# The last build of G in an encoder layer: its first load in four pieces, every second U block cut in two, 110 blocks ahead instead of 108

## Chip, cores, metric
The kernel runs on one core of one Trainium2 chip. The metric is the device time of one execution in microseconds, the median of the runs. The engines are named as in the profile: PE (TensorE, matmul), PEld (its weight loads), DVE (VectorE), ACT (ScalarE), POOL (GpSimd), SP (SyncE). A q behind the name means the engine's sequencer, which issues DMAs and waits.

## The reference
One layer of a post-norm encoder with 512 tokens of width 1024: layer norm, two kinds of attention, a second norm, and then the part that this case is about, a product-key expert layer (PEER) with 16384 experts:

```python
def one_chunk(xb):
    q = (xb @ w_q).reshape(PEER_CHUNK, PEER_HEADS, PEER_KEY_DIM)
    s1 = jnp.einsum('thd,kd->thk', q[..., :half], sub_keys[0])
    s2 = jnp.einsum('thd,kd->thk', q[..., half:], sub_keys[1])
    ...
    idx = (e1 * PEER_N_KEYS + e2).reshape(PEER_CHUNK, PEER_HEADS * PEER_TOPK)
    g = jax.nn.softmax(cv.astype(jnp.float32), axis=-1).reshape(PEER_CHUNK, -1).astype(xb.dtype)
    u = u_table[idx]
    hpre = jnp.einsum('td,ted->te', xb, u)
    act = g * jax.nn.gelu(hpre, approximate=False)
    return jnp.einsum('te,ted->td', act, v_table[idx])
```

Each token picks 128 experts. Its output is the sum of their rows of V, each weighted with a routing weight g times the gelu of the product of the token with the expert's row of U. A gate and a last norm follow.

## The kernel before, in words
**Three kinds of tokens.** The first 128 tokens are done by gathers: GpSimd fetches the picked rows of U, and later of V, one per token and pick, by indirect DMA, and VectorE multiplies them (`rows` at line 1170, `fetch_u` and `gather_v` at lines 1517 to 1536). The other 384 tokens are done densely: for all experts the activation is made and multiplied with V, and G, a matrix of routing weights with zeros where an expert wasn't picked, masks it. Of these 384, the 128 of chunk 1 (called own, NGC = 1) get their products with U by gathers too (`own_rows`), so the dense product with U runs over N_U = 256 tokens, and that with V over 384.

**Blocks.** The experts lie in 128 blocks of 128. A block of U is 512 KB. LEAD = 108 blocks of U are multiplied ahead of the loop, in FP32 (`lead_block`, line 1281: 8 matmuls of 128x256 against `whole`, the sum of the two parts of the turned tokens). Results of blocks below SPILL = 96 go to DRAM (`ge_dram`) and come back in the loop; the last ones stay in SBUF, KEPT_K of them in a pool of the gate's tiles (`leave_u`, line 1264) and the rest in the eight buffers `ge`. The remaining blocks of U are multiplied in the loop (`expert_in`, line 845): the block is loaded, split into a high part (a ScalarE copy to FP32R) and a low part (a VectorE subtraction), and 24 matmuls sum three products of parts (`mm3`, line 128).

**Building G.** For chunks 2, 3 and last chunk 1 `build_g` (line 1085) makes 128 tokens of G, in 16 steps of eight tokens: one-hots on VectorE and ScalarE, their products on PE, and ScalarE copies the sums to a stage `g_st`. A stage of 32 tokens is sent to `g_dram` in four stores (`send`, line 1068), issued from ScalarE. Four such slices belong to each chunk, 12 to all (NTG). Of the last chunk slices 0 and 1 are sent; 2 and 3 stay. The first eight blocks' worth of G for the loop is `first_g` (line 1446): its slices 0 to 3 are copied by ScalarE out of the last build's stages, its slices 4 to 11 are loaded back from `g_dram` by SyncE, in one load of 1 MB that is issued ahead of the last build. Just before it all stores that are still open are sent in a row (line 1444).

**Order of the work.** Ahead of the loop every engine's order is written out by hand. A planner keeps a balance: each build or side step returns its time on VectorE, `run_pe` (line 1076) multiplies it with PACE = 1.1 and deals out that much of PE's own work (`pe_work`: U blocks, the gate), whose pieces have planned prices (PRODUCT_U, 0.436 for one of the eight products of a block). During the last build 26 side rows (`beside`, line 1200: gathers of the first chunk, and two early blocks of V, cut into the free half of `hTh` and `hTl`) run between the build's steps. U blocks come through four buffers (three `raw`, one `raw_u`); SyncE loads the next when PE has finished with a buffer. What is left of PE's work after the build runs at line 1495, before the loop's own matmuls.

**The loop** (line 1564) takes 128 steps, blocks 96 to 127 first and then 0 to 95. Step n loads the block of V, splits it, multiplies G with the gelu results (line 1598), splits that, and adds 18 matmuls of 128x512 to six accumulators (`expert_out`, line 1546). Steps 8 to 27 also make a block of U (`block_of_u`, line 1478). Between the steps 231 remaining gather steps are dealt out by a key (lines 1626 and 1627): a step with a block of U counts 1, one without 0.57. G comes in tiles for eight steps; a tile is loaded in four pieces (`load_g`, line 1463), in steps 3 to 6 of a group of eight early in the loop and in steps 6 and 7 later:

```python
if n % GB == (GB // 2 - 1 + q if n < KEPT + 128 - LEAD + 4 else GB - 2 + q // 2):
    gt_next = load_g(n // GB * GB + GB, 3 - q if n < GB else q, gt_next, q == 0)
```

The functions that the change touches, as the profile's line numbers have them:

Of the kernel before, what the change touches and what calls it, by code (L numbers as in the profile page):

```python
# [15 lines left out]
OP = mybir.AluOpType  # L16
# [15 lines left out]
N_S = 128  # L32
# [1 line left out]
GT = 32  # L34
G_PARTS = 4
GB = 8
LEAD = 108
SPILL = 96
KEPT = 8
KEPT_K = 4  # L40
FIRST = 40
PACE = 1.1
AHEAD = 14.0
# [5 lines left out]
OWN_G_LATE = 4.0  # L49
SEAM = 7.0  # L50
WAIT = 8.4
OWN_LATE = 10.0
LATE = 0.57
OT = 8
W_SCALE = 32768.0
G_SPLIT = 1.0
# [23 lines left out]
def tile_encoder_layer(ctx: ExitStack, tc: tile.TileContext, A: dict, out: bass.AP):  # L80
# [105 lines left out]
    def flat_of(t, i, n=1):  # L186

        return t.rearrange("p a b c -> p (a b c)")[:, i * T:(i + n) * T]
# [6 lines left out]
    def ps_tile(name, bufs=2):  # L195
        return ps6.tile([128, 512], F32, name=name, bufs=bufs)
# [871 lines left out]
    def send():  # L1068

        if parts:  # L1070
            g, t, x = parts.pop(0)
            n = 128 // G_PARTS
            nc.scalar.dma_start(g_dram[g][:, x * n * GT:(x + 1) * n * GT],
                                t[:, x * n:(x + 1) * n].rearrange("p i t -> p (i t)"))

    def run_pe(amount):
        nonlocal due
        due += amount * PACE
        while due > 0:
            done = next(pe_work, 1e9)  # L1080
            due -= done
        if due < -1e6:
            due = 0.0

    def build_g(c, e1, e2, gw):
# [55 lines left out]
        for q in range(128 // OT):  # L1141
            oh = bt.tile(wide, F16, name="oh_i")
            by_v = [128, 2 * np_ - OI_ACT, 128, 2]
            nc.vector.tensor_tensor(oh[:, OI_ACT:], pairs.unsqueeze(1).to_broadcast(by_v),
                                    keys[:, q].rearrange("p s (a b) -> p (s a) b", b=2)[:, OI_ACT:].unsqueeze(2)
                                    .to_broadcast(by_v), op=OP.is_equal)
            for i in range(2 * OI_ACT):
                nc.scalar.activation(oh[:, i // 2, :, i % 2], iota, AF.Abs, bias=ne[:, OT * q + i:OT * q + i + 1])
            nc.scalar.activation(oh[:, 0:OI_ACT], oh[:, 0:OI_ACT], AF.Relu, bias=1.0, scale=-1.0)
            if ahead:  # L1150
                sums = products(*ahead)
                due -= G_SPLIT
            yield SPLIT_OH
            oj = bt.tile([128, 2, np_, 128, 2], F16, name="oh_j")
            for part in range(2):
                nc.vector.tensor_tensor(oj[:, part], oh[:, np_:],
                                        wt[:, q, part].rearrange("p (a b) -> p a b", b=2).unsqueeze(2)
                                        .to_broadcast([128, np_, 128, 2]), op=OP.mult)
                if part == 0:
                    yield SPLIT_OJ  # L1160
            if ahead:
                leave(ahead[0], sums)
            ahead = (q, oh, oj)
            yield SPLIT_OJ
# [31 lines left out]
    v_cut = {}  # L1196

    v_homes = [[flat_of(t, 2 * x, 2) for t in (hTh, hTl)] for x in range(2)]

    def beside():  # L1200

        nonlocal due
        raw = []

        def cut(n):
            split(*v_homes[n], raw[n])
            v_cut[n] = v_homes[n]

        for k, x in enumerate(rows(i_sel[:, 0, :], h[0], hdot[:, 0, :], range(BESIDE))):
            if k == BESIDE - 12:  # L1210
                due -= SEAM
            if k in (BESIDE - 12, BESIDE - 5):
                n = len(raw)
                raw.append(rw.tile([128, D], F32, name="h_s" if n else "gb"))
                nc.sync.dma_start(raw[n], v_rows[(SPILL + n) * 128:(SPILL + n + 1) * 128, :])
            yield x
            if k == BESIDE - 4:
                cut(0)
                yield 1.2
        cut(1)  # L1220
        yield 1.2


    PRODUCT_U, PRODUCT_G = 0.49 * N_U / 288, 0.69
    raws = []
    tasks = []
# [51 lines left out]

    last = []

    def lead_block():


        fill()
        if not raws:
            return
        nonlocal u_done
        i, raw = raws.pop(0)
        ps = psH.tile([128, 512], F32, name="hp") if gating else ps_tile("mm", 4)
        for k in range(8):  # L1290
            nc.tensor.matmul(ps[:, :N_U], raw[:, k], whole[:, k, :], start=(k == 0), stop=(k == 7))  # L1291
            if k == 3 and last:
                leave_u(*last.pop())
            if k % 2 and tasks:
                tasks.pop(0)()
            yield PRODUCT_U
        last.append((i, ps))
        u_done = i + 1
        if i in home_of:
            name, t = home_of[i]  # L1300
            idle[name].append(t)
# [95 lines left out]
    pe_work = gate_and_leads()  # L1397
    own, own_due = None, 0.0

    def run(steps, share=0.0, n=2):  # L1400

        nonlocal own_due
        for amount in steps:
            send()
            if amount is None:
                for _ in range(n if own else 0):
                    run_pe(next(own, 0.0))
                continue
            run_pe(amount)
            own_due += amount * share  # L1410
            while own and own_due > 0:
                x = next(own, None)
                if x is None or not x:
                    own_due = -1e9
                    break
                run_pe(x)
                own_due -= x

    with tc.manual_schedule(engines={nc.vector.engine, nc.scalar.engine, nc.tensor.engine, nc.sync.engine,
                                     nc.gpsimd.engine}):  # L1420
        fill()
        held = []
        run(route(NGC, held))
        own = own_rows(*held)
        run_pe(next(own))
        own_due = -OWN_LATE
        for c in range(NGC + 1, 4):
            res = []
            if c > NGC + 1:
                run(route(0, []), OWN)  # L1430
            run(route(c, res), OWN)
            if c > NGC + 1:
                run_pe(WAIT)
            run(build_g(c, *res), OWN)
        own_due = 1e9
        run([0.0], 1.0)
        side = beside()
        run_pe(next(side))
        for _ in own:
            pass  # L1440
        own = None
        run_pe(LAG)

        while parts:
            send()
        first_g = pX.tile([128, NTG, GB, GT], F32, name="gt1")
        nc.sync.dma_start(first_g[:, 128 // GT:].rearrange("p g i t -> p g (i t)"),
                          g_dram[128 // GT:, :, SPILL * GT:(SPILL + GB) * GT].rearrange("g p x -> p g x"))
        build = build_g(NGC, *held)
        next(build)  # L1450
        run_pe(next(side))
        own = side
        own_due = -OWN_G_LATE
        run(build, OWN_G)
        for x in own:
            run_pe(x)
        while parts:
            send()
        pb.close()
# [278 lines left out]
```

## Time and profile before

| | |
|---|---|
| median of 3 runs | 1489.74 us (1486.84 to 1492.28) |
| profiled execution, its own time | 1489.54 us |
| its span, first to last instruction | 1487.8 us |
| mean granted clock of TensorE | 0.996 |
| PE, DVE, ACT, POOL busy | 97%, 85%, 43%, 38% of the span |
| DMA | 453.82 MB, mean 305 GB/s |
| last build of G | about 810 to 878 us |
| first matmul of the loop's accumulators | 893.3 us |

The profile is one execution. A window row gives, for each engine, its busy time in the stretch with the number of instructions behind it, then the granted clock, the busy share of the 16 DMA engines and what they moved. An FP32 matmul leaves two entries in the trace, so a block of U ahead of the loop leaves 16. Entries of PE overlap, as a matmul's end is modelled: the distance of two starts tells the pace, not the duration of one. Times are microseconds from the start of the span.

### The profile page before, as it was taken

The page shows a single profiled execution, that of the slowest core. Times are in us where ns is not written, and L with a number is a line of the kernel's source. Part 1 is how long each engine was busy: PE and PEld are TensorE (multiplying, and loading weights), DVE is VectorE, ACT ScalarE, POOL GpSimd, SP SyncE. Part 2 cuts the span into 40 slices and gives each one's busy share as a digit, 9 for nine tenths or more (in the row PEclk, how much of TensorE's full clock was granted, in tenths as well). Part 3 has the DMA queues.
Part 4 walks back from the last instruction along what each step waited for, and adds up shares of the span by engine and source line. Part 5 has one row for each costly group of instructions (what it writes and reads, how often), then busy time and mean ns, then how long its engine had stood idle before and what let it go on. Part 6 is the DMA issues. An engine that isn't in the chain of part 4 may idle for free.

```text
span 1487.8 us, 22518 instructions
## 1 busy us (share of the span) xinstructions
PE 1450.2 (97%) x7693; PEld 1212.4 (81%) x7693; DVE 1268.5 (85%) x2736; ACT 638.4 (43%) x1203; POOL 570.7 (38%) x520
## 2 busy tenths in 40 slices
PE   9999999999999999999998999999999999999997
PEld 5788777788888878888887888988888888888775
DVE  7376786579998979998776987999899999999997
ACT  3355776243221554212555763444343333333433
POOL 1013110010014544344442435665555666666630
PEclk9999999999999999999999999999999999999999
DMA  7333340175239999999999999999999999999992
GB/s 255 99 111 92 97 128 30 29 245 170 100 125 351 334 416 415 405 324 336 392 416 410 376 396 369 415 417 417 401 393 411 412 412 411 412 412 412 411 362 85
DMA packets 196851, 453.82 MB, mean 305 GB/s; under 512 B 18945, under 2 KB 96897, under 8 KB 196738
## 3 DMA queue, kind: packets, MB, share of 16 engines
q1 hardware_dynamic: 119168, 211.72, 38.6%
q0 software_dynamic: 57984, 207.12, 35.5%
q10 hardware_dynamic: 19586, 33.57, 5.9%
q8 instruction: 60, 0.98, 0.2%
q14 instruction: 53, 0.43, 0.1%
HBM read 411.70 MB, written 37.75 MB: 302 GB/s over the span
## 4 chain that ended last, share of the span: by engine, by line
PE 56%; DMA 22%; DVE 9%; issue 6%; ACT 4%; POOL 3%; SPq 0%; ACTq 0%; DVEq 0%; POOLq 0%
PE acc L1551 16%; DMA raw<-in_v_rows_dram 11%; PE mm L1291 6%; PE hp L1291 5%; DMA ge_dram<-ge 4%; PE mm L129 4%; PE mm L131 4%; PE mm L130 4%; PE pj L129 3%; PE pj L130 3%; PE pj L131 3%; DMA v_raw<-in_v_rows_dram 3%; PE hp L129 1%; PE hp L131 1%; PE hp L130 1%
## 5 line engine op out<-in xcount | busy, mean ns | idle before, releaser
L110 DVE TENSOR_TENSOR wlo<-raw,whi 128x1024 fp32r<-128x1024 f32 (+4 forms) x113 | 131.5, 1164 | 45.7 <-ACT whi L110 45.4
L110 ACT CAST a_hi<-gt 128x384 fp32r<-128x384 f32 (+2 forms) x128 | 64.9, 509 | 242.4 <-DVE gt L1598 179.5
L110 ACT CAST whi<-raw 128x1024 fp32r<-128x1024 f32 (+4 forms) x113 | 113.0, 1001 | 106.9 <-PE mm L130 47.3
L1291 PE MATMUL mm<-whole,raw 128*128 128x256 f32 x672 | 153.1, 381 | 1.5 <-DMA raw<-in_uT_dram 1.5
L1174 POOL DMA_INDIRECT whi<-in_u_rows_dram,s_ix x51 | 64.2, 1259 | 218.5 <-DVE cand L994 129.7
L1551 PE MATMUL acc<-hTh,a_hi 128*128 128x512 f32 x456 | 141.8, 391 | 0.1
L1551 PE MATMUL acc<-hTl,a_hi 128*128 128x512 f32 x456 | 141.2, 390 | 0.0
L1551 PE MATMUL acc<-hTh,a_lo 128*128 128x512 f32 x456 | 140.9, 389 | 0.0
L1291 PEld LDWEIGHTS mm<-whole,raw 128*128 128x128 f32 x672 | 125.6, 190 | 17.9 <-DMA raw<-in_uT_dram 1.9
L1534 POOL DMA_INDIRECT gat<-in_v_rows_dram,i_sel x64 | 100.8, 1574 | 55.0 <-DVE base L1536 39.5
L110 ACT CAST hTh<-v_raw 128x1024 fp32r<-128x1024 f32 x74 | 77.8, 1051 | 55.9 <-PE acc L1551 23.1
L1551 PEld LDWEIGHTS acc<-hTl,a_hi 128*128 128x128 f32 x456 | 85.4, 188 | 18.3 <-DVE hTl L110 0.4
L1551 PEld LDWEIGHTS acc<-hTh,a_lo 128*128 128x128 f32 x456 | 85.4, 188 | 18.2 <-DVE a_lo L110 0.3
L1551 PEld LDWEIGHTS acc<-hTh,a_hi 128*128 128x128 f32 x456 | 84.1, 188 | 17.2 <-ACT a_hi L110 1.1
L110 DVE TENSOR_TENSOR hTl<-v_raw,hTh 128x1024 fp32r<-128x1024 f32 x74 | 90.2, 1219 | 6.4 <-ACT hTh L110 6.4
L1551 PE MATMUL acc<-wlo,a_hi 128*128 128x512 f32 x300 | 92.8, 390 | 0.2
L1551 PE MATMUL acc<-whi,a_hi 128*128 128x512 f32 x300 | 92.8, 391 | 0.1
L1551 PE MATMUL acc<-whi,a_lo 128*128 128x512 f32 x300 | 92.6, 390 | 0.0
L1174 POOL DMA_INDIRECT wlo<-in_u_rows_dram,s_ix x51 | 61.9, 1213 | 68.3 <-DVE s_dot L1176 56.0
L1519 POOL DMA_INDIRECT gat<-in_u_rows_dram,i_sel x52 | 69.1, 1329 | 45.2 <-DVE hdot L1525 34.1
L1536 DVE SCALAR_TENSOR_TENSOR base<-gat,hdot,base 128x1024 f32<-128x1024 f32 x64 | 82.0, 1281 | 1.0
L1273 ACT ACTIVATE ge<-mm 128x256 f32<-128x256 f32 x78 | 29.6, 380 | 110.4 <-PE mm L1291 100.5
(415 smaller groups left out, 3815.7 us busy)
## 6 DMA issues: line engine op xcount, KB each, us to landing
raw<-in_uT_dram SPq DMA_DIRECT2D x80, 512.0 KB, 7.8
v_raw<-in_v_rows_dram SPq DMA_DIRECT2D x78, 512.0 KB, 13.2
raw<-in_v_rows_dram SPq DMA_DIRECT2D x48, 512.0 KB, 13.8
g_dram<-g_st ACTq DMA_DIRECT2D x40, 512.0 KB, 12.1
ge_dram<-ge ACTq DMA_DIRECT2D x96, 128.0 KB, 7.0
ge<-ge_dram SPq DMA_DIRECT2D x96, 128.0 KB, 13.0
gt<-g_dram SPq DMA_DIRECT2D x30, 384.0 KB, 13.9
raw_u<-in_uT_dram SPq DMA_DIRECT2D x19, 512.0 KB, 7.8
```

What stands on the lines that cost most here:

```text
L110: cut = nc.scalar.copy(hi, src), nc.vector.tensor_tensor(lo, src, r32(hi), op=OP.subtract)
L129: nc.tensor.matmul(ps, a[0], b[0], start=start, stop=False)
L130: nc.tensor.matmul(ps, a[0], b[1], start=False, stop=False)
L131: nc.tensor.matmul(ps, a[1], b[0], start=False, stop=stop)
L1174: nc.gpsimd.indirect_dma_start(out=u[:], out_offset=None, in_=u_rows, in_offset=bass.IndirectOffsetOnAxis(ap=ix[:, k:k + 1], axis=0))
L1273: nc.scalar.activation(ge, ps[:, :N_U], AF.Gelu)
L1291: nc.tensor.matmul(ps[:, :N_U], raw[:, k], whole[:, k, :], start=(k == 0), stop=(k == 7))
L1519: nc.gpsimd.indirect_dma_start(out=u[:], out_offset=None, in_=u_rows, in_offset=bass.IndirectOffsetOnAxis(ap=i_sel[:, c, k:k + 1], axis=0))
L1534: nc.gpsimd.indirect_dma_start(out=u[:], out_offset=None, in_=v_rows, in_offset=bass.IndirectOffsetOnAxis(ap=i_sel[:, c, k:k + 1], axis=0))
L1536: nc.vector.scalar_tensor_tensor(base[c], u, hdot[:, c, k:k + 1], base[c], op0=OP.mult, op1=OP.add)
L1551: nc.tensor.matmul(acc[c][hf], a[:, cs], b[:, hf * 512:(hf + 1) * 512], start=(n == 0 and i == 0), stop=(n == 127 and i == 2))
```

## The change
Four edits.

First, the stores that are still open and the load of `first_g` are taken from before the last build. The load becomes four loads of two slices each (`load_first`), issued by SyncE at the build's steps 6, 7, 8 and 9; each first sends any store of the earlier chunks that is still open. The stores otherwise leave one per planner step.

Second, between the LAG work and the side row BESIDE - 7, every U block with an even number is split ahead of its matmuls into a high and a low part (ScalarE copy, VectorE subtraction), in the free halves of `hTh` and `hTl`, and multiplied with 24 FP32R matmuls instead of 8 FP32 ones. Its planned price per k is 0.36 instead of 0.436.

Third, LEAD is 110 instead of 108 and KEPT_K 6 instead of 4, so 18 blocks of U are left for the loop.

Fourth, each step of the last build deals out 0.1 less (MORE_G, times PACE).

```diff
-LEAD = 108
+LEAD = 110
-KEPT_K = 4
+KEPT_K = 6
+FIRST_G_AT = 6
+FIRST_PARTS = 4
+MORE_G = -0.1
+CUT_EVERY = 2
...
+    def load_first(x):
+        while parts and parts[0][0] >= N_S // GT:
+            send()
+        n = (NTG - N_S // GT) // FIRST_PARTS
+        g = slice(N_S // GT + x * n, N_S // GT + (x + 1) * n)
+        nc.sync.dma_start(first_g[:, g].rearrange("p g i t -> p g (i t)"),
+                          g_dram[g, :, SPILL * GT:(SPILL + GB) * GT].rearrange("g p x -> p g x"))
...
             nc.scalar.activation(oh[:, 0:OI_ACT], oh[:, 0:OI_ACT], AF.Relu, bias=1.0, scale=-1.0)
+            if c == NGC and 0 <= q - FIRST_G_AT < FIRST_PARTS:
+                load_first(q - FIRST_G_AT)
...
+            if k == BESIDE - 7:
+                cutting = False
...
+    def cut_next():
+        nonlocal n_cut
+        if cutting and len(raws) > 1 and raws[1][0] % CUT_EVERY == 0 and raws[1][0] not in in_parts:
+            i, raw = raws[1]
+            hi, lo = [t.rearrange("p (k n) -> p k n", n=128) for t in v_homes[n_cut % 2]]
+            n_cut += 1
+            in_parts[i] = hi, lo
+            tasks.extend([lambda: nc.scalar.copy(hi, raw), nothing, nothing, nothing,
+                          on_vector(1.2, lambda: nc.vector.tensor_tensor(lo, raw, r32(hi), op=OP.subtract))])
...
+        parts_u = in_parts.pop(i, None)
         for k in range(8):
-            nc.tensor.matmul(ps[:, :N_U], raw[:, k], whole[:, k, :], start=(k == 0), stop=(k == 7))
+            if k == 1:
+                cut_next()
+            if parts_u:
+                mm3(ps[:, :N_U], [t[:, k] for t in parts_u], (hTh[:, 1, k, :], hTl[:, 1, k, :]), k == 0, k == 7)
+            else:
+                nc.tensor.matmul(ps[:, :N_U], raw[:, k], whole[:, k, :], start=(k == 0), stop=(k == 7))
...
-            yield PRODUCT_U
+            yield PRODUCT_C if parts_u else PRODUCT_U
...
-            run_pe(amount)
+            run_pe(amount + more)
...
         run_pe(LAG)
-        while parts:
-            send()
+        cutting = True
         first_g = pX.tile([128, NTG, GB, GT], F32, name="gt1")
-        nc.sync.dma_start(first_g[:, 128 // GT:].rearrange("p g i t -> p g (i t)"),
-                          g_dram[128 // GT:, :, SPILL * GT:(SPILL + GB) * GT].rearrange("g p x -> p g x"))
...
-        run(build, OWN_G)
+        run(build, OWN_G, more=MORE_G)
```

## Rows read from the trace of the kernel before

**Rows 1.** The page, part 1: busy us, share of the span, instructions.
```profile
PE 1450.2 (97%) x7693; PEld 1212.4 (81%) x7693; DVE 1268.5 (85%) x2736; ACT 638.4 (43%) x1203; POOL 570.7 (38%) x520
```

**Rows 2.** Windows of 20 us in the loop: PE, PEld, DVE, ACT, POOL, PEclk, DMA, GB/s.
```profile
1200.00:1220.00 20.00, 20.00 (x90) 16.57 (x89) 19.79 (x24) 8.25 (x12) 13.27 (x9) 1.00 1.03 413
...
1360.00:1380.00 20.00, 19.77 (x85) 15.13 (x84) 17.78 (x21) 6.63 (x10) 10.74 (x8) 1.00 1.03 411
```

**Rows 3.** Timeline of PE, a step with a block of U and one without.
```profile
930.25 0.28 PE L129 MATMUL hp<-hTh,whi 128*128 128x256 f32 x1
...
933.13 0.63 PE L1551 MATMUL acc<-hTh,a_hi 128*128 128x512 f32 x2
...
940.11 0.63 PE L1551 MATMUL acc<-hTh,a_hi 128*128 128x512 f32 x2
...
1200.41 0.61 PE L1551 MATMUL acc<-whi,a_hi 128*128 128x512 f32 x2
...
1204.49 0.61 PE L1551 MATMUL acc<-hTh,a_hi 128*128 128x512 f32 x2
```

**Rows 4.** Windows of the last build of G, columns as in rows 2.
```profile
815.00:875.00 60.00, 54.33 (x415) 47.76 (x416) 56.01 (x88) 48.15 (x122) 23.28 (x19) 0.97 0.98 389
815.00:820.00 5.00, 3.62 (x28) 3.22 (x29) 4.93 (x9) 4.47 (x12) 0.00 (x0) 1.00 0.67 269
825.00:830.00 5.00, 3.54 (x27) 2.79 (x25) 5.00 (x10) 3.99 (x11) 2.31 (x2) 1.00 1.04 420
855.00:865.00 10.00, 7.17 (x63) 6.24 (x62) 8.88 (x16) 8.65 (x22) 3.46 (x3) 0.83 1.03 419
```

**Rows 5.** The chain of waits at the build's beginning: start, us, what.
```profile
802.15 11.03 DMA ge_dram<-ge
...
820.23 7.72 DMA raw<-in_uT_dram
```

**Rows 6.** SyncE's own waits, 780 to 905 us: total, times, longest.
```profile
SPq L1251 <- PE mm L1291: 53.3, 14, 9.8
...
SPq L1447 <- DMA g_dram<-g_st: 11.5, 1, 11.5
```

**Rows 7.** Windows of line 1291 alone, in the build and behind it: PE, PEld.
```profile
810.00:878.20 68.20, 49.51 (x212) 39.42 (x212) 0.97 0.98 387
878.20:893.30 15.10, 14.34 (x68) 12.46 (x66) 1.00 1.02 385
```

**Rows 8.** Timeline: the last two blocks of U, and the loop's first matmul.
```profile
886.58 7.07 PE L1291 MATMUL hp<-whole,raw 128*128 128x256 f32 x32
...
893.29 0.81 PE L1551 MATMUL acc<-hTh,a_hi 128*128 128x512 f32 x2
```

**Rows 9.** Groups of instructions by form: the two halves of a cut.
```profile
L110 DVE TENSOR_TENSOR wlo<-raw,whi 128x1024 fp32r<-128x1024 f32 x102 | 125.0, 1226 | 41.5 <-ACT whi L110 41.2
L110 ACT CAST whi<-raw 128x1024 fp32r<-128x1024 f32 x102 | 107.1, 1051 | 100.2 <-PE mm L130 47.3 <-DMA raw<-in_v_rows_dram 28.7 <-PE pj L130 13.9
```

**Rows 10.** Timeline of DVE amid the last build.
```profile
847.14 0.42 DVE L1598 TENSOR_TENSOR gt<-gt,g_raw 128x256 f32<-128x256 f32 x1
...
868.92 1.22 DVE L1176 CUSTOM_DVE_ANT_0 wlo<-wlo,h 128x1024 f32<-128x1024 f32 x1
```

**Rows 11.** The page, part 6: DMA issues, KB each, us to landing.
```profile
raw<-in_uT_dram SPq DMA_DIRECT2D x80, 512.0 KB, 7.8
...
gt<-g_dram SPq DMA_DIRECT2D x30, 384.0 KB, 13.9
```

**Rows 12.** SyncE's own waits, 925 to 1065 us and then 1100 to 1340 us.
```profile
SPq L1489 <- DVE hTl L110: 69.7, 17, 4.5
...
SPq L1489 <- DMA raw<-in_v_rows_dram: 43.3, 29, 2.3
```

**Rows 13.** Timeline of SyncE in the loop: a G load, and step 30's V.
```profile
1038.55 0.43 SPq L1474 DMA_DIRECT2D gt<-g_dram  x1
...
1045.19 2.18 SPq L1489 DMA_DIRECT2D v_raw<-in_v_rows_dram  x1
```

More of the change, by code (lines that the diff above doesn't have):

```diff
@@ L1198, in tile_encoder_layer @@
     v_homes = [[flat_of(t, 2 * x, 2) for t in (hTh, hTl)] for x in range(2)]
+    cutting, n_cut, in_parts = False, 0, {}
     def beside():
-        nonlocal due
+        nonlocal due, cutting
         raw = []
@@ L1221, in beside @@
         yield 1.2
+    PRODUCT_C = 0.36
     PRODUCT_U, PRODUCT_G = 0.49 * N_U / 288, 0.69
@@ L1398, in tile_encoder_layer, with run @@
     own, own_due = None, 0.0
-    def run(steps, share=0.0, n=2):
+    def run(steps, share=0.0, n=2, more=0.0):
         nonlocal own_due
```

## The prediction, made before the changed kernel ran
> **What bounds the kernel now.** I read the page first, then windows by stage, then single lines. On the page TensorE is busy 97% of the span and VectorE 85% [rows 1]; the average says nothing about a stage, so the stage that the change touches and the loop behind it were read apart. A result counts as a change here from 0.3%, about 4.5 us; that is what a measurement of this kernel can tell.
>
> The loop over 128 blocks: a window in its middle shows TensorE without a gap at 90 matmuls in 20 us, VectorE busy 19.79 of 20, and the DMA engines full at 413 GB/s [rows 2]. Three limits stand almost on top of each other. From 1360 us on there are windows with 85 matmuls instead of 90: TensorE has begun to miss its data. The instruction lines give the pace: a step with a block of U begins at 933.13 and the next at 940.11, so 6.98 us; a step without one takes 1204.49 - 1200.41 = 4.08 us [rows 3]. A block of U inside the loop costs TensorE 2.90 us, of which its 24 matmuls are 933.13 - 930.25 = 2.88 us.
>
> The last build of G (810 to 878 us): in its main 60 us TensorE is idle 60 - 54.33 = 5.67 us and VectorE 60 - 56.01 = 3.99 us; ScalarE has 11.85 us free [rows 4]. The idle time of TensorE lies in three places: 1.38 us at 815 to 820, 1.46 us at 825 to 830, and 2.83 us at 855 to 865, where the granted clock also falls (0.83 in the mean, so part of that stretch ran at 1.2 GHz after TensorE had stood still).
>
> The chain of waits explains the first two. At 802.15 a store of a spilled block starts and takes 11.03 us; ScalarE's next issue, one of three stores of G sent off in a row, waits for it, and the casts that open the build stand behind on ScalarE. Then a U block issued only at 820.23 lands 7.72 us later, and TensorE waits for it [rows 5]. It was late because SyncE stood 11.5 us at the load of the first G, which waits for G's stores; otherwise its loads of U wait for buffers that TensorE frees [rows 6].
>
> After the build TensorE has U blocks left and nothing else: a block of U ahead of the loop is recorded as 16 entries, and there are 212 in the build (13.25 blocks) and 68 behind it (4.25 blocks) [rows 7]. Two of the last take 893.29 - 886.58 = 6.71 us, 3.35 each [rows 8]. So up to 893.3 us the total work of TensorE plus its idle time sets the start of the loop.
>
> **The change, part by part.**
> *Two more blocks ahead.* Each adds 8 FP32 matmuls of 3.35 us together: +6.70 us of TensorE before the loop. Its load (512 KB) and gelu only move. KEPT_K only gives two results another home; no instruction is added, so nothing. In the loop 18 steps have a block of U instead of 20: 2 x 2.90 = -5.80 us of TensorE; each also takes a load from SyncE, a copy of 1.05 us from ScalarE and a subtraction of 1.23 us from VectorE [rows 9].
>
> *Every second block cut.* Cutting is on from the end of the LAG work until the twentieth row of the side work, which VectorE does at 868.92 [rows 10]. Counted back from 107, the 280 entries put the build's beginning in the middle of block 90; the twentieth row falls in block 101. An even block is picked two blocks ahead, so 94, 96, 98, 100 and 102: five. Each is then 24 matmuls on FP32R parts instead of 8 in FP32: 2.88 instead of 3.35 us, so 5 x 0.47 = -2.35 us. The Trainium skill (FP8 and Floating Point Precision, TensorE Precision Notes) says that true FP32 is four passes; three products of one pass would then be 2.51 us, an estimate, the five would save 4.2 us, and the sum would end 1.85 us lower. The rows say 2.88, and that is used.
>
> The price is on the other engines: 5 x 1.05 = 5.3 us on ScalarE, which has 11.85 us free, and 5 x 1.23 = 6.1 us on VectorE, which has 3.99 free. Both are set at nothing, because the order hands TensorE 1.32 us of U work for each cut: it works while the build gets longer. Without that cover the surplus of VectorE, 2.1 us, is idle time of TensorE. A copy also waits for its U block, with the build's one-hots queued behind it on ScalarE; landing takes 7.8 us [rows 11], and as a cut block frees its buffer early, the load is some two blocks ahead (68.2 us over 13.25 blocks are 5.1 us each [rows 7], so 10 us). Only the first cut is short of that.
>
> *The first G in four pieces, and no stores in a row.* The three stores now leave one per step, behind the opening casts on ScalarE; the load passes the U loads on SyncE and comes between them at steps 6 to 9, when its stores have long landed. This takes away the two causes above: 1.38 + 1.46 = -2.8 us of idle time. Bounds: nothing (the idle time comes back later in the build, since ScalarE and VectorE have more to do) and 5.67 (all goes). I take 2.8, the two places with a named cause; what is late next is the 855 to 865 place, where ScalarE waits for its own stores. Four issues instead of one cost SyncE about 1 us, hidden, as it waits for buffers most of the time [rows 6].
>
> *MORE_G.* 50 steps get 0.11 us less of TensorE's work each, -5.5; the five cuts hand out +6.6 and cost the planner 3.0 less. So the build holds 4.1/3.48 = 1.2 blocks more, and 4.25 + 2 - 1.2 = 5.05 blocks are left behind it. This moves work and is nothing by itself.
>
> *In the loop, beside the blocks.* The same 231 gather steps are dealt out by a new key: 231 x 0.57/76.7 = 1.717 per ordinary step instead of 1.698. At 0.52 MB each this is 0.010 MB, 0.024 us at 412 GB/s; over some 90 steps 2.1 us if the transfers bound the loop, 0 if TensorE does. In the stretch with U SyncE mostly waits for VectorE to free buffers (69.7 us), later for earlier transfers (43.3 us) [rows 12]: late in the loop transfers do count. I take 1.0.
>
> A side effect: the test that switches the G loads to their later steps compares with KEPT + 128 - LEAD + 4, which falls from 32 to 30. At steps 27, 28 and 29 three pieces of the next G are loaded, and at 30 and 31 the tile is opened anew and all four are loaded. That is 0.92 MB twice (2.2 us at 412 GB/s), and SyncE must wait for the third piece, issued at 1038.55 in the trace of before, before it comes to step 30's rows of V at 1045.19 [rows 13]. A G load takes 13.9 us to land [rows 11], so SyncE stands some 7 us longer. Bounds 0 and 2.2; I take 0, as this falls where SyncE is ahead and waits for buffers.
>
> **The sum.** Ahead of the loop 6.70 - 2.35 - 2.8 = +1.55; in it -5.80 + 1.0 = -4.80; together -3.25 us. The profiled execution took 1489.54 us (span 1487.8), 0.2 below the median of 1489.74. 1489.54 - 3.25 = **1486.3 us**.
>
> **The rivals.**
> *A, all idle time goes.* The build gets U work enough that TensorE never stands, and the transfers cost nothing: 6.70 - 2.35 - 5.67 - 5.80 = -7.1, 1482.4 us. For it: 1.2 blocks more are dealt into the build. Against it: VectorE has less than 4 us to spare. Chance 0.20.
>
> *B, the loop is bound by bytes.* Then two blocks of U taken out give back 1.05 MB, 2.5 us at 412 GB/s, not 5.8: +1.55 - 2.5 = -0.95, 1488.6 us. For it: DMA is full all the way and TensorE misses data after 1360. Against it: 90 matmuls in 20 us before that is TensorE's own pace. Chance 0.17.
>
> *C, slower: VectorE is held for the last piece of G.* In the trace of before the loop's very first multiplication with G stands on VectorE amid the build, at 847.14 [rows 10]. It reads the slices that now come in pieces at build steps 6 to 9, the last at about 810 + 68.2 x 10/16 = 853 us. If it keeps a place soon behind that issue, VectorE waits for the landing, the build's one-hots queue behind it, and TensorE's products wait for those. The price is between 7.8 us (a U load) and 13.9 (a G load) [rows 11]; nearer to the first, which is of the same stretch: 9. That gives 1495.3 us. It decides on whether that multiplication is placed before some 860 us. Chance 0.13.
>
> The forecast itself, give or take the half-microsecond terms, has 0.50.
>
> **How the numbers follow.** Low is rival A, 1482.4. High is the forecast with no idle time won (+2.8) and both transfer costs in full (+3.3): 1492.4. Below 1485.2 it is faster by over 0.3%: all of A and some of the forecast's half, 0.34. Above 1494.2: most of C and a little of B and the forecast with every cost at its upper bound, 0.12. The rest, 0.54, is within 0.3%.
>
> **What would show it.** Right: the first accumulation of the loop begins at about 895 us (893.29 before); no idle of TensorE at 815 to 820 and 825 to 830; five groups of 24 matmuls in the build, 2.88 us each; 18 steps of 6.98 us; seven G loads at steps 27 to 31 instead of four. Rival A: the loop begins by 892. Rival B: fewer windows with 90 matmuls after 1100 us. Rival C: VectorE idle some 9 us before the multiplication with G, released by a load of G. The forecast is wrong if the loop begins after 898, or if the loop is not 3 us shorter.

## The result: 0.8% slower, and the profile after

Before 1490.23 us median (1486.84 to 1493.36, 7 runs), after 1501.18 us (1496.96 to 1507.29, 7 runs). The ratio is 1.0081, with a 95% interval of 1.0066 to 1.0096: some 12 us slower, where 3.3 us faster was forecast and the range ended at 1492.4. (The quotient of the two medians is 1.0073, 11 us; the ratios here and below are those on record, which are not quotients of medians.) The profiled execution took 1504.03 us, its span is 1502.3 us (1487.8 before) and its mean granted clock 0.989 (0.996).

The page's first part, as [rows 1]: every engine works a little more, but TensorE's 4 us cannot explain 14.5 us of span.

```profile
PE 1454.3 (97%) x7725; PEld 1217.3 (81%) x7725; DVE 1273.5 (85%) x2740; ACT 641.7 (43%) x1209; POOL 575.2 (38%) x520
```

So the first question is where the time lies. The timeline of PE gives two marks: the loop's first matmul, and the starts of steps 24 and 25.

```profile
905.92 0.81 PE L1584 MATMUL acc<-hTh,a_hi 128*128 128x512 f32 x2
...
1050.43 0.63 PE L1584 MATMUL acc<-hTh,a_hi 128*128 128x512 f32 x2
...
1057.29 0.28 PE L135 MATMUL hp<-hTh,wlo 128*128 128x256 f32 x1
1061.96 1.22 PE L1584 MATMUL acc<-hTh,a_hi 128*128 128x512 f32 x2 [4.39 <-ACT a_hi L114]
```

The loop starts at 905.92, 12.63 us later than in [rows 8]. From there to step 26 it takes 165.84 us instead of 158.50: 7.34 us, all of it around step 25, which starts 11.53 us after step 24 instead of 6.98. From step 26 to step 127 it takes 416.13 us instead of 421.53, so 5.40 us less. 12.63 + 7.34 - 5.40 = 14.57, which is the difference of the spans, 14.50, but for 0.07 us at the end.

**Ahead of the loop.** Windows of the last build in the changed kernel, columns as in [rows 2]; the last row is of the loop:

```profile
810.00:895.00 85.00, 74.43 (x567) 67.74 (x566) 67.65 (x102) 61.38 (x142) 27.70 (x23) 0.92 0.93 343
815.00:820.00 5.00, 4.59 (x43) 3.99 (x41) 4.96 (x7) 4.14 (x9) 1.42 (x1) 1.00 1.03 416
825.00:830.00 5.00, 1.91 (x16) 1.72 (x15) 3.97 (x7) 2.76 (x6) 1.42 (x2) 0.89 1.01 390
830.00:835.00 5.00, 5.00 (x32) 5.00 (x31) 4.92 (x8) 3.85 (x10) 1.74 (x2) 0.50 0.61 186
865.00:870.00 5.00, 0.88 (x9) 0.54 (x6) 2.60 (x5) 4.59 (x12) 0.16 (x1) 0.98 1.02 418
870.00:875.00 5.00, 3.62 (x32) 3.18 (x32) 5.00 (x8) 3.51 (x8) 2.15 (x2) 0.50 1.03 419
1060.00:1080.00 20.00, 18.04 (x79) 15.16 (x80) 17.68 (x29) 8.51 (x15) 9.67 (x7) 0.83 0.94 338
```

The same 85 us of the kernel before:

```profile
810.00:895.00 85.00, 79.32 (x544) 69.35 (x543) 70.59 (x113) 58.63 (x145) 28.13 (x24) 0.98 0.98 384
```

The place at 815 to 820 was won as forecast (4.59 us busy, 3.62 in [rows 4]). But TensorE now idles 10.57 us instead of 5.68, and behind two of the gaps the granted clock is 0.50 for 5 us, that is 1.2 GHz. The timeline of PE shows the longest single wait in either gap:

```profile
829.82 1.86 PE L1128 MATMUL tr<-oh_i,oh_j 128*128 128x128 f16 x16 [3.10 <-ACT g_st L1141]
...
868.48 0.23 PE L1128 MATMUL tr<-oh_i,oh_j 128*128 128x128 f16 x1 [2.84 <-DVE oh_j L1171]
```

The chain of waits names what each gap waited for:

```profile
821.26 6.94 DMA raw_u<-in_uT_dram
828.23 1.04 ACT hTh L1308
...
838.88 6.50 DMA raw<-in_uT_dram
845.40 0.33 ACTq L1077
...
857.43 9.88 DMA gt<-g_dram
867.40 0.26 DVE gt L1631
```

First, ScalarE's copy for a cut (L1308) waits for a block of U issued only at 821.26, with the build's work queued behind it. Second, an issue of a store of G on ScalarE comes behind another landing of U, and the one-hots after it are 4.93 us late. The trace's records say how the two are tied: the DMAs that SyncE and ScalarE issue take eight completion semaphores in turn. The store at 845.40 has the one of the load of U issued at 838.88, and waits for that load's landing; in the kernel before, a store issued at 813.21 waits in the same way for the one that began at 802.15 [rows 5]. Third, VectorE stands at the loop's first multiplication with G (L1631) until the last of the four pieces has landed: rival C. The timeline of VectorE, then SyncE's issues of that piece and the load ahead of it:

```profile
861.81 0.95 DVE L1157 TENSOR_TENSOR oh_i<-ne,eT 128x1536 f16<-128x1536 f16 x1
867.40 0.43 DVE L1631 TENSOR_TENSOR gt<-gt,g_raw 128x256 f32<-128x256 f32 x1 [4.64 <-DMA gt<-g_dram]
867.74 0.68 DVE L1171 TENSOR_TENSOR oh_j<-oh_i,eT 128x1024 f16<-128x1024 f16 x1
```

```profile
847.53 0.46 SPq L1086 DMA_DIRECT2D gt<-g_dram  x1
857.05 0.33 SPq L1270 DMA_DIRECT2D raw<-in_uT_dram  x1
857.43 0.55 SPq L1086 DMA_DIRECT2D gt<-g_dram  x1
```

The last piece leaves 0.38 us behind a load of U that had to wait until TensorE freed its buffer; the three before it were away by 847.53.

**In the loop.** The waits at 1040 to 1075 us (engine, what it was about to do, what it waited for; total, times, longest), then ScalarE's timeline there, and SyncE's:

```profile
ACT gt L1506 <- DMA gt<-g_dram: 12.0, 1, 12.0
DVE a_lo L114 <- ACT a_hi L114: 10.9, 1, 10.9
...
PE acc L1584 <- ACT a_hi L114: 4.4, 1, 4.4
```

```profile
1060.78 0.71 ACT L1506 COPY gt<-g_st 128x256 f32<-128x256 f32 x2 [11.97 <-DMA gt<-g_dram]
1061.40 0.51 ACT L114 CAST a_hi<-gt 128x384 fp32r<-128x384 f32 x1
```

```profile
1046.53 1.33 SPq L1626 DMA_DIRECT2D ge<-ge_dram  x1
1060.77 0.89 SPq L1507 DMA_DIRECT2D gt<-g_dram  x2
```

L1506 is ScalarE's copy of the two kept slices into the tile of G that is opened a second time. The tile is only free when the loads of its first opening have landed; in the trace's records the copy waits for all three, issued at 1038.41, 1040.00 and 1044.91. SyncE stands there, as forecast, but so does ScalarE; and in ScalarE's order these copies stand ahead of the split of step 25. TensorE waits 4.39 us for that split and then runs at half clock: the 18 matmuls of step 25 take 6.70 us from first to last start instead of 3.88. The spans of two matmuls in the fence with the marks (1.22 us against 0.63) show it as well. The Trainium skill (TensorE: Matmul & The Clock Gate, Part 1) lists two states for the clock gate that sets this clock by TensorE's activity, half rate and full rate. The trace agrees: every value recorded in it is 0.50 or 1.00, and the values between them above are means over a window.

### The profile page after: what moved, and what is told of

It reads as the page before. It is cut to its first block, busy times and chain, and to the rows that moved or that the text cites. A ratio compares the mean times of both kernels' runs of the same rounds, so it can differ in the third digit from the quotient of the medians.

```text
span 1502.3 us, 22600 instructions
## 1 busy us (share of the span) xinstructions
PE 1454.3 (97%) x7725; PEld 1217.3 (81%) x7725; DVE 1273.5 (85%) x2740; ACT 641.7 (43%) x1209; POOL 575.2 (38%) x520
## 4 chain that ended last, share of the span: by engine, by line
PE 63%; DVE 12%; DMA 11%; issue 6%; POOL 4%; ACT 3%; SPq 0%; ACTq 0%; POOLq 0%; DVEq 0%
PE acc L1584 28%; PE mm L1327 7%; PE mm L133 4%; PE mm L135 3%; PE mm L134 3%; PE pj L133 3%; PE hp L1327 3%; PE pj L134 3%; DMA gt<-g_dram 3%; PE pj L135 3%; DMA raw<-in_uT_dram 2%; DMA raw<-in_v_rows_dram 2%; DMA ge_dram<-ge 2%; POOL wlo L1189 2%; POOL whi L1189 1%
## 5 line engine op out<-in xcount | busy, mean ns | idle before, releaser
L1327 PE MATMUL mm<-whole,raw 128*128 128x256 f32 x656 | 149.2, 381 | 0.0
L114 DVE TENSOR_TENSOR a_lo<-gt,a_hi 128x384 fp32r<-128x384 f32 (+2 forms) x128 | 69.6, 545 | 22.6 <-ACT a_hi L114 22.5
```

Source lines behind the costliest of these rows:

```text
L114: cut = nc.scalar.copy(hi, src), nc.vector.tensor_tensor(lo, src, r32(hi), op=OP.subtract)
```

## The experiments

Each is given with its change against the changed kernel or the kernel before. The theory: the doubled G load costs the loop some 7 us, and ahead of the loop the hold of VectorE by the last piece and cut copies that wait for U cost another 8. The rivals: the cuts' own work lengthens the build, or two more blocks ahead cost more than they give.

### The doubled load of G

The test below is the switch: from the step it names on, loads of G are issued in their later places. Against the changed kernel, the switch at step 32 as before:

```diff
-if n % GB == (GB // 2 - 1 + q if n < KEPT + 128 - LEAD + 4 else GB - 2 + q // 2):
+if n % GB == (GB // 2 - 1 + q if n < 32 else GB - 2 + q // 2):
```

> The changed kernel with one edit: the test that switches the loads of G to their later steps compares with 32 again, so no piece is loaded twice. Theory (the second opening of the tile holds ScalarE's copy into it for 12 us, the split of step 25 stands behind that copy, and TensorE is then slow for a step): the loop gets back nearly all of the 7.3 us that it lost between step 0 and step 26, so about 1494.2 us, steps 24 and 25 start 6.98 us apart, and the granted clock in 1060 to 1080 us is 1.0. Rival (the two extra U blocks or the gathers upset the loop there anyhow): within 1.5 us of the changed kernel, 1501 us, and the gap of step 25 stays. The start of the loop is the same in both, near 906 us.

Measured 1499.8 us (1497.94 to 1505.83, 4 runs), ratio 1.0084 (1.0058 to 1.0111). In the trace the theory holds: steps 24 and 25 start 6.98 us apart, step 26 comes 158.48 us after step 0, and from the loop's first matmul to that of step 127 it takes 575.88 us instead of 581.97. The median doesn't show it. So both were run once more, on one chip:

> The changed kernel itself, on the same chip as the next run: 1500 to 1502 us; step 25 late by more than 4 us, and a hold of VectorE for the last piece of the first G.

> The changed kernel with the switch of G's loads at step 32 again, a second time and beside the changed kernel. Theory (its first median was high because the stalls ahead of the loop, which it shares, happened to be long in those few executions): 5 to 7 us below the changed kernel on this chip, about 1495 us. Rival (with VectorE held ahead of the loop the second opening costs the median nothing): within 2 us of it.

The changed kernel took 1500.87 us (1.0070, 1.0052 to 1.0088); with the switch at 32, 1498.41 us (1490.60 to 1506.65; 1.0059, 1.0039 to 1.0079). The loop's part was again shorter, 576.31 against 580.65 us, while the loop started at 907.09 against 905.01. So in the two pairs of traces the loop starts 1.0 and 2.1 us later with the switch at 32, though the code ahead of it is the same in both, and that takes back part of the 6.1 and 4.3 us won in the loop. The intervals of the ratios overlap; the medians alone leave it open.

The same edit by itself, on the kernel before, where the build is steady:

```diff
-if n % GB == (GB // 2 - 1 + q if n < KEPT + 128 - LEAD + 4 else GB - 2 + q // 2):
+if n % GB == (GB // 2 - 1 + q if n < 30 else GB - 2 + q // 2):
```

> The kernel before, with one number changed: the switch of G's loads at step 30 instead of 32, so the tile for steps 32 to 39 is opened at step 27 and again at step 30. Theory: the whole cost of the second opening shows here by itself, 7 us: about 1495.5 us, step 25 starts 11 us or more after step 24 and the clock falls to 0.5 behind it. Rival (it needs the other edits): less than 2 us, 1488.5 to 1490.5.

1492.69 us, ratio 1.0028 (1.0016 to 1.0039): 4.2 us by the ratio, less than expected, but the mechanism is there. ScalarE's timeline, then PE's:

```profile
1050.73 0.71 ACT L1473 COPY gt<-g_st 128x256 f32<-128x256 f32 x2 [10.36 <-DMA gt<-g_dram]
1051.35 0.51 ACT L110 CAST a_hi<-gt 128x384 fp32r<-128x384 f32 x1
```

```profile
1051.91 1.22 PE L1551 MATMUL acc<-hTh,a_hi 128*128 128x512 f32 x2 [2.82 <-ACT a_hi L110]
```

Here it is step 26 that comes late: the steps from 25 to 27 take 18.56 us instead of 13.96, so 4.6 us more, and the price is smaller than in the changed kernel: TensorE stands 2.82 us instead of 4.39, and the 18 matmuls behind it take 1.62 us longer than 3.88, not 2.82.

### The first G, earlier, as before, and the cuts taken out

The pieces at build steps 2 to 5 instead of 6 to 9:

```diff
-FIRST_G_AT = 6
+FIRST_G_AT = 2
```

> The changed kernel with the four pieces of the first G at build steps 2 to 5 instead of 6 to 9, so the last has landed well before VectorE's multiplication with it. Theory (VectorE is held 4.6 us at that multiplication, TensorE stands behind it and then runs at half clock, some 6 us in all): loop start near 900 us, time about 1495, no half clock at 870 to 875 us. Rival (the build is bound by VectorE and ScalarE work anyhow): the wait goes and the time stays within 1.5 us of 1501. A third (the pieces now stand on SyncE at the stores of the chunk before, and U blocks come late again): idle time of TensorE at 815 to 830 us, time about 1499.

1494.90 us, ratio 1.0050 (1.0031 to 1.0069). The loop starts at 894.30 instead of 905.92. VectorE reaches the multiplication at 842.12 and waits for nothing, and TensorE's idle time is back to 4.43 us:

```profile
842.12 0.42 DVE L1631 TENSOR_TENSOR gt<-gt,g_raw 128x256 f32<-128x256 f32 x1
```

```profile
810.00:895.00 85.00, 80.57 (x611) 73.11 (x610) 73.62 (x111) 64.32 (x151) 27.57 (x23) 0.98 1.00 384
```

This prices the place of the pieces, 4.6 us by the ratios (6.3 by the medians). It doesn't price the hold by itself, since the other two gaps shrink with it.

The first G as in the kernel before (the stores in a row and one load ahead of the build), the rest as changed:

```diff
-            if c == NGC and 0 <= q - FIRST_G_AT < FIRST_PARTS:
+            if c == NGC and False:
                 load_first(q - FIRST_G_AT)
...
+        while parts:
+            send()
         first_g = pX.tile([128, NTG, GB, GT], F32, name="gt1")
+        nc.sync.dma_start(first_g[:, 128 // GT:].rearrange("p g i t -> p g (i t)"),
+                          g_dram[128 // GT:, :, SPILL * GT:(SPILL + GB) * GT].rearrange("g p x -> p g x"))
```

> The changed kernel with the first G as before: the open stores in a row and one load ahead of the build. Cuts, 110 blocks and the second opening of the tile stay. Theory: the hold of VectorE at about 862 us goes (6 us with its slow clock) and the two stalls at the build's head come back (2.8 us), so about 1498 us and a loop start near 903. Rival (late pieces cost nothing, head stalls were worth winning): about 1504. If the cuts wait for late U blocks here too, there is one more stall near 830 us than in the kernel before, and the time stays near 1501.

1502.85 us, 1.0097 (1.0080 to 1.0114): the theory missed, and the case of late U blocks came nearest. VectorE is not held (its multiplication is at 849.7), but a cut's copy now waits 7.1 us for a block of U, since SyncE's loads of U stand behind that of G. TensorE is busy 2.56 and 1.10 of the 5 us from 820 and from 825 on. ScalarE's timeline, and the second of these windows:

```profile
824.66 1.04 ACT L1308 CAST hTh<-raw 128x1024 fp32r<-128x1024 f32 x1 [7.14 <-DMA raw<-in_uT_dram]
```

```profile
825.00:830.00 5.00, 1.10 (x11) 1.09 (x11) 4.26 (x6) 4.18 (x10) 0.76 (x1) 0.50 1.01 396
```

So cuts and late loads of U don't go together, which the prediction had set at nothing.

The cuts never switched on, the rest as changed:

```diff
-        cutting = True
+        cutting = False
```

> The changed kernel with the cutting never switched on: no U block is split, all are FP32. TensorE gets 5 x 0.47 = 2.35 us more work. Theory (two of the cut copies wait on ScalarE for a block of U that has not landed, with the build's one-hots behind them, and that costs about 5 us with the slow clock that follows): the loop starts 2 to 3 us earlier than in the changed kernel, about 1498.5 us, and TensorE is without the half clock at 830 to 835 us. Rival (the cuts only save TensorE's work; the stalls have other causes): about 1503.5 us. A third (the 11 us of cuts on two busy engines lengthen the build): the build's last product comes 5 us or more earlier and the time is about 1497.

1510.64 us, 1.0151 (1.0134 to 1.0168), slower than every theory said. Without the cuts other work stands on the queues: the last piece is issued at 848.08, VectorE comes to its multiplication 11 us ahead of its landing, and ScalarE stands 7.86 us at a store that has the semaphore of another piece. The timelines of VectorE, ScalarE and PE:

```profile
862.39 0.42 DVE L1631 TENSOR_TENSOR gt<-gt,g_raw 128x256 f32<-128x256 f32 x1 [10.96 <-DMA gt<-g_dram]
```

```profile
859.61 1.31 ACT L1161 ACTIVATE oh_i<-iota,eT 128x128 f16<-128x128 f32 x4 [7.86 <-DMA gt<-g_dram]
```

```profile
862.39 1.87 PE L1128 MATMUL tr<-oh_i,oh_j 128*128 128x128 f16 x16 [9.48 <-ACT g_st L1141]
```

It doesn't price the cuts. It is a second case of the hold, more than twice as long, but here ScalarE's wait for a piece ends TensorE's longest gap. The loop of the profiled execution starts at 908.95, 3.0 us later than in the changed kernel, of which the six blocks that stay in FP32 explain 2.8 (six times 0.47); the median is 9.5 us higher.

### Both faults out, and then each term

Pieces at steps 2 to 5 (FIRST_G_AT = 2) and the switch at step 32 (`n < 32`), the two diffs above together:

> The changed kernel with both suspected faults taken out: the first G's pieces at build steps 2 to 5, and the switch of G's loads at step 32 again. Theory (the two costs are independent: about 6 us each, of the hold ahead of the loop and of the second opening in it): 1494.9 - 7 = 1488 us, no difference from the kernel before that can be told; the loop starts near 894 us and takes 158.5 us to step 26. Rival (the timed runs with the second opening removed came out no lower than those with it, so it costs the median nothing): 1494 to 1495 us.

1488.71 us, 0.9998 (0.9988 to 1.0008): level with the kernel before, so the place of the pieces and the switch together account for the 12 us. Against the pieces moved alone (1.0050) the switch gives back 6 to 8 us here, and the medians agree with the traces. The same without cuts (`cutting = False`):

> The same with no block cut. Theory (with VectorE no longer held, cuts pay what TensorE saves, 0.47 us a block): 2 to 3 us slower than with cuts, about 1490.5 us, loop start near 897. Rival (cuts lengthen the build by their work on VectorE and by copies that wait for U): 2 to 4 us faster, about 1485. Without cuts the planner deals out less of U inside the build, so more blocks are left behind it; that alone moves nothing if TensorE has no idle time.

1492.16 us, 1.0018 (1.0006 to 1.0031): the cuts are worth some 3 us where loads of U come early (3.0 by the ratios, 3.4 by the medians). There are six of them in the trace, not five; six times 0.47 is 2.8. And with 108 blocks ahead instead of 110:

```diff
-LEAD = 110
-KEPT_K = 6
+LEAD = 108
+KEPT_K = 4
-FIRST_G_AT = 6
+FIRST_G_AT = 2
```

> Cuts and pieces at steps 2 to 5, but 108 blocks ahead as in the kernel before (and so the switch at step 32 by itself). By the prices used (6.70 us for two blocks ahead, 5.80 us in the loop): 0.9 us less than with 110, about 1487 us, with the loop starting near 887.5 us. Rival (two blocks ahead are worth more because the loop's transfers also get lighter): 1 to 3 us more than with 110.

1487.01 us, 0.9992 (0.9976 to 1.0008), a median 1.7 us below the variant with 110. That is what the terms gave for the two blocks, 0.9 to 1.9, but the intervals overlap and it isn't shown.

Two attempts to get more out of this variant. One hands out 0.1 more per build step (MORE_G 0), the other cuts every block (CUT_EVERY 1):

```diff
-MORE_G = -0.1
+MORE_G = 0.0
```

```diff
-CUT_EVERY = 2
+CUT_EVERY = 1
```

> 108 blocks ahead, pieces at steps 2 to 5, every second block cut, and each build step handing out 0.1 more (MORE_G 0), so about 1.3 blocks more stand in the build and as many less behind it. Theory (TensorE still stands some 5 us in the build for want of work): 1 to 2 us faster than 1487.0 us. Rival (its idle time is waits for one-hots and stages, which more U work only delays): no difference, or up to 2 us slower.

> 108 blocks ahead, pieces at steps 2 to 5, and every block cut instead of every second, some 12 instead of six. Theory (cuts paid 3.4 us for six, a little more than the 2.8 us that TensorE saves): 2 to 3 us faster than 1487.0 us. Rival (VectorE is then full; 6 more cuts are 7.4 us of its work and 6.3 us of ScalarE's): the build is longer, 2 us slower or more.

The first took 1497.08 us, 1.0053 (1.0038 to 1.0068), outside both the theory and the rival. Its timelines of SyncE, VectorE, ScalarE and PE:

```profile
826.71 9.47 SPq L1270 DMA_DIRECT2D raw<-in_uT_dram  x2
836.27 0.70 SPq L1086 DMA_DIRECT2D gt<-g_dram  x1
```

```profile
845.33 0.43 DVE L1631 TENSOR_TENSOR gt<-gt,g_raw 128x256 f32<-128x256 f32 x1 [3.44 <-issue]
```

```profile
848.48 1.04 ACT L1308 CAST hTh<-raw_u 128x1024 fp32r<-128x1024 f32 x1 [5.33 <-DMA raw_u<-in_uT_dram]
```

```profile
895.26 1.24 PE L1584 MATMUL acc<-hTh,a_hi 128*128 128x512 f32 x4 [2.39 <-ACT hTh L114]
```

A change of 0.1 in a planner's number moved the fourth piece behind two loads of U again, and the hold came back: the view names no releaser, but in the records VectorE waits until 845.28 for the semaphore of that piece. The next load of U went out behind it, and a cut's copy waited 5.33 us for it; TensorE's longest wait in the build, 4.12 us, ends with ScalarE's work queued behind that copy. And with fewer blocks left behind the build, TensorE reached the loop before its first block of V was cut. Steps 0 to 8 then took 37.87 us instead of 32.86. The second took 1509.29 us, 1.0143 (1.0122 to 1.0164). There are 15 cuts, and only two homes for their parts, so copies wait for TensorE and TensorE for copies. It stood still for 16.3 of 85 us, and steps 0 to 8 took 37.97 us:

```profile
ACT hTh L1308 <- PE mm L134: 11.1, 7, 4.1
...
PE mm L135 <- DVE hTl L1309: 5.1, 4, 1.6
```

### Each edit alone, on the kernel before

Three kernels, each with one edit of the change alone. The first is the changed kernel with 108 blocks, no cuts, MORE_G 0 and the pieces at steps 2 to 5:

```diff
-LEAD = 110
+LEAD = 108
-KEPT_K = 6
+KEPT_K = 4
-FIRST_G_AT = 6
+FIRST_G_AT = 2
-MORE_G = -0.1
+MORE_G = 0.0
...
-        cutting = True
+        cutting = False
```

> The kernel before with the first G's edit alone: four pieces at build steps 2 to 5, no row of stores, no cuts, 108 blocks, MORE_G 0. By the prediction's step: 2.8 us of idle time go, 1486 us. Rival (the idle time comes back elsewhere in the build, or the last piece still holds VectorE): no gain, 1488 to 1491 us, TensorE still idle 5 to 6 us between 810 and 895 us.

The second has the cuts and MORE_G -0.1, with 108 blocks and the first G in one load ahead of the build (the diff of that experiment above, LEAD 108, KEPT_K 4):

> The kernel before with the cuts alone (and MORE_G -0.1, which goes with them); first G as before, 108 blocks. By the prediction's step: six cuts of 0.47 us, 2.8 us less, 1486 us. Rival (with the loads of U late after the first G's load, as in the kernel before, the cuts' copies wait for U on ScalarE and hold the build): 2 to 6 us slower than the kernel before, 1491 to 1495 us.

The third is the kernel before with

```diff
-LEAD = 108
-KEPT_K = 4
+LEAD = 110
+KEPT_K = 6
...
-if n % GB == (GB // 2 - 1 + q if n < KEPT + 128 - LEAD + 4 else GB - 2 + q // 2):
+if n % GB == (GB // 2 - 1 + q if n < 32 else GB - 2 + q // 2):
```

> The kernel before with 110 blocks ahead and KEPT_K 6 alone, the switch of G's loads kept at step 32. By the prediction's steps: 6.70 - 5.80 = +0.9, and up to 1.0 for the gathers: 1490 to 1491 us. Rival (the loop wins more than TensorE's 5.80, as its transfers get lighter): 1488 us or less.

Together with the switch alone they give a price for each edit:

| edit alone | ratio (95%) | that is, of 1489 us | term of the prediction |
|---|---|---|---|
| first G in pieces, steps 2 to 5 | 0.9994 (0.9981 to 1.0008) | -0.9 | -2.8 |
| cuts, with MORE_G -0.1 | 1.0036 (1.0022 to 1.0050) | +5.4 | -2.35 |
| 110 blocks ahead, switch at 32 | 1.0026 (1.0012 to 1.0041) | +3.9 | +0.9 and 1.0 |
| switch at 30 | 1.0028 (1.0016 to 1.0039) | +4.2 | 0 |

The pieces alone do what was forecast in the profiled execution: TensorE idles 2.70 us instead of 5.68, and the loop starts 3.5 us earlier:

```profile
810.00:895.00 85.00, 82.30 (x563) 71.88 (x562) 70.51 (x113) 58.64 (x145) 30.73 (x27) 1.00 1.02 399
```

The median, 1487.04 us against 1489.71, has 2.7 us of it, the ratio 0.9, with an interval from -2.8 to 1.2; so neither the whole gain nor none is ruled out. The cuts alone lose, for the reason seen above; the first copy stands on ScalarE with the gelu, the one-hots and the stage behind it (timeline of ScalarE, and a window):

```profile
825.47 1.04 ACT L1308 CAST hTh<-raw 128x1024 fp32r<-128x1024 f32 x1 [7.18 <-DMA raw<-in_uT_dram]
826.42 0.38 ACT L1292 ACTIVATE ge<-mm 128x256 f32<-128x256 f32 x1
```

```profile
825.00:830.00 5.00, 0.28 (x4) 0.28 (x4) 3.45 (x5) 4.09 (x9) 0.00 (x0) 0.74 1.02 406
```

The lead alone costs more than its terms: the loop starts 8.3 us later (6.70 forecast) and its own part is 4.0 us shorter (5.8 forecast). The later start has the clock beside it: 0.96 in the mean of 810 to 895 us against 0.98. The four sum to +12.6, near the whole, but that is no proof of the split: in the changed kernel the pieces come at steps 6 to 9.

### A version ahead of both

The variant with 108 blocks, pieces at steps 2 to 5 and cuts of every second block, again:

> The fastest variant again: 108 blocks, pieces at build steps 2 to 5, every second block cut. Theory: 1 to 2 us faster than the kernel before, 1487 to 1488 us, which the measurement may just tell. Rival: no difference.

1488.01 us (12 runs), ratio 0.9984 (0.9973 to 0.9995); its first measurement gave 0.9992 (0.9976 to 1.0008). So pieces at steps 2 to 5, every second block cut and 108 blocks ahead is faster than the kernel before by about 2 us (the first interval still includes no difference, the second just not), and by some 13 us than the changed one. It is less than the 0.3% that the prediction called a change.

## Why the prediction was wrong, point by point

**The doubled load of G: the step that failed outright.** It was seen, with its steps and its wait of SyncE, and set at 0 of 0 to 2.2 us, "as this falls where SyncE is ahead and waits for buffers". The load's bytes and SyncE's wait do cost nothing: V was there in time, as the steps from 26 on start 4.1 us apart as before. But `load_g` also issues two copies on ScalarE into the opened tile, and these were not counted, although every instruction of a moved step should be. They wait 12.0 us, the split of step 25 waits behind them, and the loop lost 7.3 us (4.6 in the trace and 4.2 by the ratio on the kernel before).

**Rival C's hold happened too, at a chance of 0.13.** Its mechanism was right: the multiplication kept its place, VectorE reached it at 862.76, and the last piece landed at 867.3. The price was sized by the whole time of a landing (9 us), and the range, to 1492.4, left out the 1495.3 that it gives. VectorE waited 4.64 us; TensorE stood 2.84 us at most behind it and then ran at half clock. The piece was expected to leave at about 853 us; it left at 857.43, behind a load of U that waits for TensorE to free a buffer. That queue was named for the rest of the argument and not for this. Moving the pieces to steps 2 to 5 took the hold away, with most of the other idle time of that stretch, and gave 4.6 us by the ratios; what the hold costs by itself is not shown.

**The idle time: -2.8 failed in the sum.** The two named places were read rightly; alone, the pieces take 2.98 us of idle time out of the profiled execution, and 0.9 (ratio) to 2.7 us (median) off the time. In the changed kernel the second place was filled again by the cuts' own waits (825 to 830: 1.91 us busy, 3.54 in [rows 4]). In the version with both faults out TensorE still idles 6.00 us in 810 to 895:

```profile
810.00:895.00 85.00, 79.00 (x604) 71.99 (x603) 72.40 (x110) 62.83 (x149) 27.62 (x23) 0.98 1.00 377
825.00:830.00 5.00, 1.85 (x24) 1.77 (x23) 4.51 (x6) 3.24 (x8) 1.16 (x1) 1.00 1.03 398
```

The forecast of -3.25 without this term is -0.45, and that version came out at 0.9998.

**The cuts: size right, cover wrong.** Six blocks instead of five, with 24 matmuls spaced 0.12 us, 2.88 in all, at full clock; so the rows' price held and not the estimate from the page of the Trainium skill. Where U's loads are early the cuts give some 3 us. But "Only the first cut is short of that" was a remark without a price, and not right: in the changed kernel the second copy waited, 2.21 us, and in the runs with the first G as before the first one waited 7.1 to 7.2 us, longer than VectorE's whole surplus of 2.1 us, which had been the bound.

**Two blocks ahead, and the loop.** The change in the loop's remainder was -5.40, against -5.80 + 1.0 forecast; of the 18 steps with a block of U all but 24 and 25 take about 6.98 us. Ahead of the loop +12.63 is +6.70, less six cuts of 0.47 (-2.82), plus 4.89 of idle time; the 3.86 left over are matmuls at half clock, for which the two windows at 0.50 leave room. This was worked out, not tried by itself. Alone on the kernel before, the two blocks cost 3.9 us, where 0.9 to 1.9 was forecast.

**MORE_G: "nothing by itself" was wrong.** It decides whether the fourth piece comes ahead of a held load of U, and whether blocks of U are left to cover the first cuts of V; in the one variant where it was tried its 0.1 is worth 9 to 10 us.

Left open: whether the time falls by the 4 to 6 us of the traces when the doubled load is removed from the changed kernel, where the medians fell by 1.4 and 2.5 us; and how much of the loss ahead of the loop belongs to each of the three gaps, since moving the pieces changed them all.

## What to carry to other kernels

When a constant moves a load, list what the function that issues it puts on every engine, and ask of each in-order queue what stands behind the instruction that will wait; here two small copies on an engine busy 43% of the time cost more than 0.92 MB of transfers. A load that is issued late "because it is needed late" must be checked against the place of its first reader in the hand-written order and against the held loads that it queues behind. An issue can also wait for a DMA that it has nothing to do with, the one that had its semaphore before it, so a DMA more or less changes what later issues wait for. A work-balance constant in such an order is also a placement: run each edit alone before they are tuned together.

## What was not expected of the hardware

A gap in TensorE's work could cost 1.6 times its length here. After 4.39 us without work at step 25 the 18 matmuls took 2.82 us longer, most of them at a granted clock of 0.50; the two gaps in the build, with 3.10 and 2.84 us as their longest single waits, were each followed by 5 us at 0.50. The length of a wait alone doesn't tell: in the version with both faults out TensorE waited 3.15 us up to 828.32, and the clock stayed at 1.00 from 825 to 835, while waits of 1.11 and 1.72 us lie in the stretch of 855 to 865 whose mean is 0.83 [rows 4]. Profiled executions also vary ahead of the loop far more than in it: the version ahead of both started its loop at 888.17 us in one and at 891.70 in the other, and took 158.48 us from there to step 26 in both.
